# Feed-forward of a two-batch encoder: the last SiLU and product of every first and third chunk are issued behind the next chunk's first copy

## The chip, the cores and the metric

The kernel runs on one core of a Trainium2 chip. The metric is the device time of one execution in microseconds (us). Its engines work side by side, each through its own instructions in a fixed order: TensorE (PE, with its weight loads as PEld), VectorE (DVE), ScalarE (ACT), GpSimd (POOL) and SyncE (SP, which here issues loads).

## The reference, cut to what matters

Two request batches of 512 and 256 tokens (768 rows together, 1024 columns) pass through a trunk of two layers in float32. Each layer is a feed-forward, a token mixer and another feed-forward, so there are four feed-forwards; all share weights between the batches.

```python
def swiglu_ffn(x, w1, w2):                    # w1: 1024 x 5632, w2: 2816 x 1024
    gate, up = jnp.split(x @ w1, 2, axis=-1)
    return (jax.nn.silu(gate) * up) @ w2

for li in range(2):
    x = x + 0.5 * swiglu_ffn(rmsnorm(x, norm_g[li, 0]), ffn_w1[li, 0], ffn_w2[li, 0])
    x = x + mixer(rmsnorm(x, norm_g[li, 1]))  # layer 0: gated recurrence, layer 1: windowed attention
    x = x + 0.5 * swiglu_ffn(rmsnorm(x, norm_g[li, 2]), ffn_w1[li, 1], ffn_w2[li, 1])
```

## The kernel before, in words

Every float32 operand is split into a high part that TensorE takes whole and a low rest, and each product of two operands is three matmuls. The high part of a weight is written by ACT (L203, `CAST w<-wr`), the low part by DVE (L204). Weights are loaded by SP into raw buffers (`wr`); sums of weights are made there too, some by DVE (L217), some by a DMA that adds, issued by POOL (L145, `into`).

The 2816 hidden columns of a feed-forward are 22 chunks of 128. Two are computed plainly (`up_plain`). The rest go through `up_pair`, which computes a chunk's gate and up parts for both halves of the tokens (384 each) with seven products instead of eight, in the order p1, p7, p2, p5, p4, p6, p3. A product is twelve matmuls of 384 columns (L422), summed in one of four PSUM banks a, b, c, d. Behind p1, ACT copies bank a to SBUF (L439), since p2 then goes on summing into the same bank: the first matmul of p2 waits for that copy. Behind p7, ACT copies bank c (L442). At the chunk's end p3 goes to bank d, DVE adds it (L459), ACT takes the SiLU (L460), DVE multiplies (L461), and the result `w` is the chunk's hidden value for the second half of the tokens.

Four chunks make a group. There are five groups in a feed-forward; in group 0 the first two chunks are the plain ones, and two more chunks stand behind the last group. Within a group the chunks go two by two: after each two, `gather` mixes their four values (L351 to L355) and splits the results (L267 on ACT, L268 on DVE). The value `w` of the first chunk of two is read by nothing before that mix, which comes after the second. Behind the four chunks `down_quad` multiplies by the second weights (L486, matmuls of 512 columns, seven products of 18 matmuls), and DVE adds each bank to the residual (L508), which frees the bank.

A recording layer turns this into one order of instructions for each engine. It moves work forward by its own rules; `issue_after(x)` makes what is recorded inside it stand behind `x` on x's engine.

Of the kernel before, what the change touches and what calls it, by code (L numbers as in the profile page):

```python
# [12 lines left out]
AF = mybir.ActivationFunctionType  # L13
# [35 lines left out]
class Trunk:  # L49
    def __init__(self, ctx, tc, consts):  # L50
        self.tc, self.nc = tc, tc.nc
        pool = lambda name, **kw: ctx.enter_context(tc.tile_pool(name=name, bufs=1, **kw))
        self.cp = pool("consts")
        self.xp = pool("xp")
        self.wp = pool("wp")
        self.tp = pool("tp")
        self.sp = pool("stats")
        self.ap = pool("arena")
        self.pp = pool("psum", space=bass.MemoryType.PSUM)
        self.dp = pool("dram", space=bass.MemoryType.DRAM)  # L60
        self.uid = 0
        self.deferred = []
        self.queue, self.loaded, self.staged, self.held = [], [], {}, 0
        self.setup(consts)

# [362 lines left out]
                    skip_group_check=True,  # L428
                )

    def up_pair(self, tag, j):
        nc = self.nc
        key = (tag, j)
        a, b, c, d = (self.ps(H) for _ in range(4))
        v, w, t = (self.tmp(H) for _ in range(3))
        p = lambda name, ps, first, last: self.product(key, name, FACTOR[name], ps, first, last)
        free = lambda *names: [self.done((*key, name)) for name in names]
        p("p1", a, True, False)
        nc.scalar.copy(v, a)  # L439
        free("p1")  # L440
        p("p7", c, True, False)
        nc.scalar.copy(w, c)  # L442
        free("p7")
        p("p2", a, False, True)
        nc.scalar.activation(a, a, AF.Silu)
        free("p2")
        p("p5", d, True, False)
        nc.vector.tensor_sub(w, w, d)
        free("p5")
        p("p4", c, False, True)  # L450
        p("p6", b, True, True)
        nc.vector.tensor_sub(v, v, b)
        nc.vector.tensor_sub(t, c, v)
        nc.vector.tensor_mul(t, t, a)  # L454
        free("p4", "p6")
        yield t
        nc.vector.tensor_sub(w, w, v)
        p("p3", d, False, True)
        nc.vector.tensor_add(v, v, d)  # L459
        self.last_act = nc.scalar.activation(v, v, AF.Silu).ins  # L460
        self.last_dve = nc.vector.tensor_mul(w, v, w).ins  # L461
        free("p3")
        yield w

# [45 lines left out]
    def ffn(self, tag, next_row):  # L510
        for g in range(GROUPS):
            hid = {}

            def put(name, src, kp):
                if name not in hid:
                    hid[name] = self.big([P, 2, 2, H], F32R)
                self.split(src, hid[name][:, kp, 0, :], hid[name][:, kp, 1, :])

            def gather(ts, kp):
                self.mix(ts[0], ts[1], ts[2], ts[3], lambda name, src: put(name, src, kp))  # L520

            if g == 0:
                ts = {}
                for half in range(2):
                    for j in range(PLAIN):
                        t = ts[2 * j + half] = self.up_plain(tag, j, half)
                        name = f"b{j}{half}"
                        if name != "b01":
                            put(name, t, 0)
                gather(ts, 0)  # L530
                self.run_later(len(self.deferred))
            for kp in range(2):
                if g == 0 and kp == 0:
                    continue
                ts = []
                for j in range(2):
                    for half, t in enumerate(self.up_pair(tag, 4 * g + 2 * kp + j)):
                        ts.append(t)
                        name = f"b{j}{half}"
                        if name != "b01":  # L540
                            put(name, t, kp)
                gather(ts, kp)
            self.down_quad(tag, g, hid)
        hids = []
        for j in range(NF - 2, NF):
            hid = self.big([P, 2, T], F32R)
            for half, t in enumerate(self.up_pair(tag, j)):
                self.split(t, *(hid[:, i, half * H : (half + 1) * H] for i in range(2)))
            hids.append(hid)
        if next_row is None:  # L550
            self.load_final()
        banks = {}

        def add(b, k, hid):
            sl = slice(b * P, (b + 1) * P)
            for c in range(2):
                wh, wl = self.take((tag, "last", c))
                if k == 0:
                    banks[(b, c)] = self.ps()
                w = wh[:, k, :], wl[:, k, :]  # L560
                self.mm3(banks[(b, c)], (hid[:, 0, sl], hid[:, 1, sl]), w, k == 0, k == 1)
                if b == NBLK - 1 and k:
                    self.done((tag, "last", c))

        for b in range(NBLK):
            for i, k in (((0, 0), (1, 0), (0, 1)), ((1, 1),))[b] if b < 2 else ((b, 0), (b, 1)):
                add(i, k, hids[k])
            for c in range(2):
                self.add_x(self.x[b][:, c * 512 : (c + 1) * 512], banks[(b, c)], 0.5)
            self.after_block(b, next_row)  # L570
            if b >= 4:
                self.run_later()
# [552 lines left out]
class Unit:  # L1125
# [103 lines left out]
    def finish(self):  # L1229
        lo = self.off + self.b * P  # L1230
        self.k.split(self.po.rearrange("p (c q) -> p c q", c=2), *(t[:, :, lo : lo + P] for t in self.of()))
# [114 lines left out]
```

## Time and profile before

| what | value |
|---|---|
| median of 3 runs | 2763.64 us (2762.39 to 2764.43) |
| the profiled execution | 2764.33 us, its span 2762.5 us |
| granted TensorE clock | 0.999 |
| instructions | 44483 |
| PE busy, PEld busy | 99%, 90% of the span |
| DVE, ACT, POOL busy | 76%, 48%, 11% |

The span is the time from the first to the last instruction of the profile; 1.8 us of the profiled execution lie around it. A matmul's end is modelled, and successive matmuls overlap in the profile, so the row of PE hides short stops; PEld is the row of the weight loads, which run one behind the other where TensorE doesn't wait.

### The profile page before, as it was taken

The numbers are of one execution on the slowest core, as the hardware profiler recorded it, in microseconds if no ns is written. First come the engines' busy times: TensorE is split into PE (matmuls) and PEld (weight loads), VectorE is DVE, ScalarE is ACT, GpSimd is POOL, SyncE is SP. The second block draws the span as 40 slices with busy tenths as digits, with TensorE's granted clock in tenths as the row PEclk, the third lists the DMA queues.
The fourth block names the chain that finished last, engine by engine and source line by source line (L and its number), as shares of the span: only waits on it lengthen the run. The fifth ranks groups of instructions, "written<-read, shape, count | busy, mean of one in ns | idle before, by whom it ended". The sixth has DMA issues, their size and how long they took to land.

```text
span 2762.5 us, 44483 instructions
## 1 busy us (share of the span) xinstructions
PE 2735.5 (99%) x17281; PEld 2481.5 (90%) x17281; DVE 2102.6 (76%) x3662; ACT 1326.6 (48%) x2479; POOL 309.4 (11%) x315
## 2 busy tenths in 40 slices
PE   8999999999999999999999999999999999999998
PEld 8999999888888889999999999999886789999997
DVE  7888788557477568777888878887846768788877
ACT  7444444456466354443446444444546654443444
POOL 1111211000000001121111112111000001221111
PEclk9999999999999999999999999999999999999999
DMA  5544554321110324465444355544512123555443
GB/s 160 135 117 116 138 134 119 118 67 40 55 47 25 122 62 114 112 143 133 118 120 109 83 131 138 133 115 115 146 53 77 47 62 81 134 137 128 120 112 107
DMA packets 330116, 291.63 MB, mean 106 GB/s; under 512 B 11608, under 2 KB 257840, under 8 KB 329904
## 3 DMA queue, kind: packets, MB, share of 16 engines
q1 hardware_dynamic: 294064, 212.43, 25.8%
q0 software_dynamic: 31680, 62.93, 13.4%
q10 hardware_dynamic: 4160, 13.42, 1.4%
q8 instruction: 135, 2.21, 0.3%
q14 instruction: 77, 0.63, 0.1%
HBM read 216.39 MB, written 9.44 MB: 82 GB/s over the span
## 4 chain that ended last, share of the span: by engine, by line
PE 85%; DVE 10%; ACT 3%; issue 2%; DMA 0%; DVEq 0%; ACTq 0%; SPq 0%
PE ps L422 32%; PE ps L486 21%; PE ps L262 9%; PE ps L263 9%; PE ps L264 9%; DVE w L204 2%; DVE big L268 2%; PE ps L682 1%; PE ps L1218 1%; PE ps L1157 1%; PE ps L827 1%; PE ps L1209 1%; ACT w L203 1%; DVE wr L217 1%; PE ps L324 1%
## 5 line engine op out<-in xcount | busy, mean ns | idle before, releaser
L422 PE MATMUL ps<-big,w 128*128 128x384 f32 x6720 | 1174.6, 335 | 3.4 <-ACT tA L439 2.7
L422 PEld LDWEIGHTS ps<-big,w 128*128 128x128 f32 x6720 | 1165.4, 188 | 10.9 <-ACT tA L439 9.1
L203 ACT CAST w<-wr 128x512 fp32r<-128x512 f32 x600 | 415.3, 707 | 699.8 <-DVE wr L217 376.3
L204 DVE TENSOR_TENSOR w<-wr,w 128x512 fp32r<-128x512 f32 (+1 forms) x520 | 452.8, 874 | 180.1 <-ACT w L203 153.9
L486 PE MATMUL ps<-w,big 128*128 128x512 f32 x2520 | 575.9, 389 | 1.2 <-DVE x L508 1.2
L486 PEld LDWEIGHTS ps<-w,big 128*128 128x128 f32 x2520 | 472.4, 188 | 99.6 <-ACT big L267 1.6
L508 DVE SCALAR_TENSOR_TENSOR x<-ps,x 128x512 f32<-128x512 f32 x468 | 303.5, 680 | 10.5 <-PE ps L264 10.0
L145 POOL DMA_DIRECT2D s<-wr x120 | 105.0, 875 | 1667.5 <-DMA wr<-in_ffn_w_dram 784.5
L262 PE MATMUL ps<-w,big 128*128 128x512 f32 x624 | 252.5, 405 | 0.3
L264 PE MATMUL ps<-w,big 128*128 128x512 f32 x624 | 244.6, 392 | 0.9 <-DVE big L331 0.9
L263 PE MATMUL ps<-w,big 128*128 128x512 f32 x624 | 244.4, 392 | 0.0
L262 PE MATMUL ps<-big,w 128*128 128x384 f32 (+2 forms) x640 | 219.2, 344 | 2.1 <-ACT big L267 1.3
L267 ACT CAST big<-tA 128x384 fp32r<-128x384 f32 x296 | 148.0, 513 | 149.3 <-DVE tA L454 69.0
L263 PE MATMUL ps<-big,w 128*128 128x384 f32 (+2 forms) x640 | 216.4, 338 | 0.9 <-DVE big L268 0.6
L264 PE MATMUL ps<-big,w 128*128 128x384 f32 (+2 forms) x640 | 215.6, 337 | 0.0
L268 DVE TENSOR_TENSOR big<-tA,big 128x384 fp32r<-128x384 f32 x296 | 183.0, 629 | 12.7 <-ACT big L267 11.6
L171 DVE TENSOR_TENSOR w<-wr,w 128x1024 fp32r<-128x1024 f32 x92 | 111.8, 1221 | 79.0 <-ACT w L170 73.1
L262 PEld LDWEIGHTS ps<-w,big 128*128 128x128 f32 x624 | 117.2, 188 | 29.3 <-issue 6.0
L170 ACT CAST w<-wr 128x1024 fp32r<-128x1024 f32 x92 | 96.5, 1052 | 97.8 <-PE ps L263 77.8
L204 POOL TENSOR_TENSOR w<-wr,w 128x512 fp32r<-128x512 f32 x80 | 123.3, 1541 | 177.5 <-ACT w L203 156.4
L264 PEld LDWEIGHTS ps<-w,big 128*128 128x128 f32 x624 | 117.1, 188 | 27.6 <-DVE big L331 1.7
L263 PEld LDWEIGHTS ps<-w,big 128*128 128x128 f32 x624 | 117.4, 188 | 21.8 <-issue 0.4
(163 smaller groups left out, 2899.6 us busy)
## 6 DMA issues: line engine op xcount, KB each, us to landing
wr<-in_ffn_w_dram SPq DMA_DIRECT2D x264, 512.0 KB, 3.9
s<-in_ffn_w_dram SPq DMA_DIRECT2D x120, 256.0 KB, 3.3
s<-wr POOLq DMA_DIRECT2D x120, 256.0 KB, 4.5
wr<-wr POOLq DMA_DIRECT2D x80, 256.0 KB, 3.7
wr<-in_hg_w_in_dram SPq DMA_DIRECT2D x40, 512.0 KB, 3.8
wr<-wr POOLq DMA_DIRECT2D x20, 512.0 KB, 4.6
spill<-x ACTq DMA_DIRECT2D x12, 512.0 KB, 2.7
x<-spill ACTq DMA_DIRECT2D x12, 512.0 KB, 3.3
```

The costliest lines, as they stand in the source:

```text
L145: self.nc.gpsimd.dma_start(out, src, accum_op=ALU.add)
L171: self.nc.vector.tensor_sub(lo, raw, hi.bitcast(F32))
L203: nc.scalar.copy(h, src)
L204: low = (eng or nc.vector).tensor_sub(l, src, h.bitcast(F32)).ins
L262: nc.tensor.matmul(out, a[0], b[0], start=first, stop=False)
L263: nc.tensor.matmul(out, a[0], b[1], start=False, stop=False)
L264: nc.tensor.matmul(out, a[1], b[0], start=False, stop=last)
L267: self.nc.scalar.copy(hi, src)
L268: self.nc.vector.tensor_sub(lo, src, hi.bitcast(F32))
L422: self.nc.tensor.matmul(ps, a[x], b[y], start=first and k == 0 and i == 0, stop=k == 3 and i == 2, skip_group_check=True,)
L486: nc.tensor.matmul(ps, a[x], w[y], start=name == chain and kp == 0 and q == 0, stop=kp == 1 and q == 2, skip_group_check=True,)
L508: self.nc.vector.scalar_tensor_tensor(x, ps, c, x, ALU.mult, ALU.add)
```

## The change

`up_pair` gets an argument `hold`, true for the first chunk of each two in a group (the first and third of four; in group 0 the third alone). With it the SiLU and the product (L460, L461 before) are not recorded at the chunk's end but by the next call of `up_pair`, directly behind its first copy, and the SiLU is made to stand behind that copy on ACT. That is 9 chunks in each feed-forward, 36 in the kernel. What is computed stays the same.

```diff
-    def up_pair(self, tag, j):
+    def up_pair(self, tag, j, hold=False):
...
         p("p1", a, True, False)
-        nc.scalar.copy(v, a)
+        turned = nc.scalar.copy(v, a).ins
         free("p1")
+        if self.tail:
+            self.tail(turned)
+        self.tail = None
         p("p7", c, True, False)
...
         p("p3", d, False, True)
         nc.vector.tensor_add(v, v, d)
-        self.last_act = nc.scalar.activation(v, v, AF.Silu).ins
-        self.last_dve = nc.vector.tensor_mul(w, v, w).ins
+
+        def finish(after=None):
+            with self.tc.issue_after(after) if after else nullcontext():
+                self.last_act = nc.scalar.activation(v, v, AF.Silu).ins
+            self.last_dve = nc.vector.tensor_mul(w, v, w).ins
+
+        if hold:
+            self.tail = finish
+        else:
+            finish()
         free("p3")
         yield w
...
-                    for half, t in enumerate(self.up_pair(tag, 4 * g + 2 * kp + j)):
+                    for half, t in enumerate(self.up_pair(tag, 4 * g + 2 * kp + j, j == 0)):
```

On ACT, where the fourth chunk of group 2 begins in the first feed-forward, there stood before (tA are temporaries in SBUF, ps PSUM banks, w and wr split and raw weights, big split operands of the down products):

```order
L203 CAST w_2315<-wr_2262 128x1024
L267 CAST big_1987<-tA_2162 128x384
L460 ACTIVATE tA_2160<-tA_2160 128x384
L439 COPY tA_2299<-ps_2295 128x384
L442 COPY tA_2300<-ps_2297 128x384
L203 CAST w_2345<-wr_2264 128x1024
L445 ACTIVATE ps_2295<-ps_2295 128x384
```

The same place now, where the new lines shift line numbers (L440 is the copy L439 of before, L467 the SiLU, L446 the second copy, L268 and L204 the casts L267 and L203):

```order
L204 CAST w_2313<-wr_2262 128x1024
L268 CAST big_1987<-tA_2162 128x384
L440 COPY tA_2297<-ps_2293 128x384
L467 ACTIVATE tA_2160<-tA_2160 128x384
L446 COPY tA_2298<-ps_2295 128x384
L204 CAST w_2345<-wr_2264 128x1024
L449 ACTIVATE ps_2293<-ps_2293 128x384
```

The SiLU and the copy have changed places, and nothing else. On ACT, where the second chunk of the same group begins, there stood before (`s` is the buffer in which a DMA adds two weights):

```order
L267 CAST big_1987<-tA_1879 128x384
L460 ACTIVATE tA_1877<-tA_1877 128x384
L439 COPY tA_2013<-ps_2009 128x384
L203 CAST w_2029<-s_278_1866 128x512
L442 COPY tA_2014<-ps_2011 128x384
```

and now:

```order
L268 CAST big_1987<-tA_1879 128x384
L440 COPY tA_2011<-ps_2007 128x384
L204 CAST w_2027<-s_278_1866 128x512
L467 ACTIVATE tA_1877<-tA_1877 128x384
L446 COPY tA_2012<-ps_2009 128x384
```

Here the SiLU has moved past the copy and past one cast of a weight. DVE at this second place had before:

```order
L268 TENSOR_TENSOR big_1987<-tA_1879,big_1987 128x384
L461 TENSOR_TENSOR tA_1878<-tA_1877,tA_1878 128x384
L204 TENSOR_TENSOR w_2029<-s_278_1866,w_2029 128x512
L204 TENSOR_TENSOR w_2045<-wr_1862,w_2045 128x512
L448 TENSOR_TENSOR tA_2014<-tA_2014,ps_2012 128x384
```

and has now:

```order
L269 TENSOR_TENSOR big_1987<-tA_1879,big_1987 128x384
L205 TENSOR_TENSOR w_2027<-s_278_1866,w_2027 128x512
L468 TENSOR_TENSOR tA_1878<-tA_1877,tA_1878 128x384
L205 TENSOR_TENSOR w_2045<-wr_1862,w_2045 128x512
L452 TENSOR_TENSOR tA_2012<-tA_2012,ps_2010 128x384
```

The product has moved behind one subtraction of a weight. That is so at 19 of the 36 places; at the other 17 DVE's order is unchanged. The orders of PE, POOL and SP are the same in both kernels.

More of the change, by code (lines that the diff above doesn't have):

```diff
@@ L438, in up_pair @@
         p("p1", a, True, False)
-        nc.scalar.copy(v, a)
+        turned = nc.scalar.copy(v, a).ins
         free("p1")
+        if self.tail:
+            self.tail(turned)
+        self.tail = None
         p("p7", c, True, False)
```

## The prediction

> **What bounds the kernel now.** I read the page first, then who waited for whom, then three places by time. In the page's rows of engines and of costly groups (count, then busy us, mean ns, idle us and what ended it) TensorE is the bound:
>
> ```profile
> span 2762.5 us, 44483 instructions
> PE 2735.5 (99%) x17281; PEld 2481.5 (90%) x17281; DVE 2102.6 (76%) x3662; ACT 1326.6 (48%) x2479; POOL 309.4 (11%) x315
> L422 PE MATMUL ps<-big,w 128*128 128x384 f32 x6720 | 1174.6, 335 | 3.4 <-ACT tA L439 2.7
> L422 PEld LDWEIGHTS ps<-big,w 128*128 128x128 f32 x6720 | 1165.4, 188 | 10.9 <-ACT tA L439 9.1
> ```
>
> So a gain must come from stops of PE, and the change touches one kind of stop only: p2's first matmul waiting for the copy L439. The waits of PE and of its weight loads give its size (us in total, times, longest), and the one other wait that matters below:
>
> ```profile
> PE ps L422 <- ACT tA L439: 2.7, 11, 0.4
> PEld ps L422 <- ACT tA L439: 9.1, 19, 0.8
> PE ps L486 <- DVE x L508: 1.2, 1, 1.2
> ```
>
> **What a stop costs.** Here is the start of the fourth chunk of group 2, first feed-forward (start, duration, idle time before it and who ended that):
>
> ```profile
> 247.20 0.52 ACT L267 CAST big<-tA 128x384 fp32r<-128x384 f32 x1 [0.46 <-DVE tA L454]
> 247.74 0.55 DVE L459 TENSOR_TENSOR tA<-tA,ps 128x384 f32<-128x384 f32 x1
> ...
> 248.32 0.53 ACT L460 ACTIVATE tA<-tA 128x384 f32<-128x384 f32 x1 [0.61 <-DVE tA L459]
> ...
> 248.75 0.46 ACT L439 COPY tA<-ps 128x384 f32<-128x384 f32 x1
> 249.21 0.48 ACT L442 COPY tA<-ps 128x384 f32<-128x384 f32 x1
> 249.27 10.38 PEld L422 LDWEIGHTS ps<-big,w 128*128 128x128 f32 x60 [0.47 <-ACT tA L439]
> 249.27 10.69 PE L422 MATMUL ps<-big,w 128*128 128x384 f32 x60 [0.15 <-ACT tA L439]
> 249.59 1.06 ACT L203 CAST w<-wr 128x1024 fp32r<-128x1024 f32 x1
> 249.81 0.55 DVE L461 TENSOR_TENSOR tA<-tA,tA 128x384 f32<-128x384 f32 x1
> 250.85 0.88 POOL L145 DMA_DIRECT2D wr<-wr  x1 [10.89 <-ACT w L203]
> ```
>
> ACT is done with L267 at 247.72, then stands idle 0.61 us because the SiLU is next and DVE's L459 ends only at 248.29. The copy's bank was ready long before (p7's twelve matmuls, 2.1 us, lie between p1 and the p2 that is due at 248.96 by the next lines, so p1 ended near 246.9); it starts behind the SiLU and ends at 249.21; p2 starts 0.06 later. The pace of matmuls is (10.38 - 0.19) / 59 = 0.173 us, while one lasts 0.335 in the profile, so the last matmul before the stop began at 249.27 - 0.15 - 0.335 = 248.79, the next was due at 248.96, and the stop costs 0.31 us: PE's idle time plus 0.16, or the load's idle time minus 0.16. Over all stops that is 9.1 - 19 x 0.16 = 6.1 us. PE's own row counts only the 11 longer ones, 2.7 + 11 x 0.16 = 4.5, which leaves about 0.2 for each of the eight short ones; the sum of 6.1 is consistent and I take it.
>
> The Trainium skill bears on this choice of row: "Perfetto Trace Analysis", section "Identifying the Most-Contended Engine", says that the busy share of matmuls is a poor measure because they are pipelined, and that the busy share of weight loads should be used. Taken literally the gain would be all 9.1 us. The trace agrees with half of it: the matmul row does understate (0.15 for 0.31), but the load row overstates by as much (0.47).
>
> **The change, part by part.** *The copy goes ahead of the SiLU.* It can start when ACT ends L267, at 247.72, and ends 0.46 later at 248.18. PE's p2 is due at 248.96, so 0.78 us are to spare and the stop goes. I take the 19 stops of the row to have this cause, since all wait for the same line. Price: -6.1 us, and its bounds are 4.5 (the eleven that PE's row counts) and 9.1 (all idle time of the loads).
>
> *The SiLU goes behind the copy.* In this place it needs L459, which ends at 248.29, after the copy. So it starts at 248.32 as before, ends at 248.85, and L442, whose product p7 now ends unstopped (its copy can start about 249.14), doesn't wait for it. L461 on DVE stood behind a longer subtraction anyway. Price 0.
>
> *Where the second chunk follows the first* there is no stop today:
>
> ```profile
> 218.15 0.55 DVE L459 TENSOR_TENSOR tA<-tA,ps 128x384 f32<-128x384 f32 x1
> 218.27 0.51 ACT L267 CAST big<-tA 128x384 fp32r<-128x384 f32 x1 [1.63 <-DVE tA L454]
> ...
> 218.73 0.53 ACT L460 ACTIVATE tA<-tA 128x384 f32<-128x384 f32 x1
> 219.16 0.46 ACT L439 COPY tA<-ps 128x384 f32<-128x384 f32 x1
> 219.22 0.55 DVE L268 TENSOR_TENSOR big<-tA,big 128x384 fp32r<-128x384 f32 x1
> 219.52 0.62 ACT L203 CAST w<-s 128x512 fp32r<-128x512 f32 x1
> 219.69 0.55 DVE L461 TENSOR_TENSOR tA<-tA,tA 128x384 f32<-128x384 f32 x1
> ...
> 220.17 0.69 DVE L204 TENSOR_TENSOR w<-s,w 128x512 fp32r<-128x512 f32 x1
> ```
>
> The copy moves to 218.78, the cast to about 219.2, the SiLU to 219.8 with its end at 220.3. DVE does the subtraction (220.17) 0.4 us earlier and the product (219.69) 0.6 us later; the two add up to the same busy time. The DMAs of SP and POOL that reuse `s` wait for that subtraction, so they come earlier if anything. Nothing reads the product before the mix, a whole chunk later. Price 0; its bounds are 0 and the 0.6 us that the third rival takes.
>
> *What is late next.* With PE 0.31 us earlier from p2 on, the down stage begins earlier, but the chain that feeds it does not:
>
> ```profile
> 253.76 0.55 DVE L448 TENSOR_TENSOR tA<-tA,ps 128x384 f32<-128x384 f32 x1 [0.80 <-PE ps L422]
> 255.57 1.05 ACT L203 CAST w<-wr 128x1024 fp32r<-128x1024 f32 x1 [3.42 <-DMA wr<-wr]
> 256.66 1.23 DVE L204 TENSOR_TENSOR w<-wr,w 128x1024 fp32r<-128x1024 f32 x1 [2.35 <-ACT w L203]
> 257.92 0.55 DVE L452 TENSOR_TENSOR tA<-tA,ps 128x384 f32<-128x384 f32 x1
> 259.80 4.51 PE L486 MATMUL ps<-w,big 128*128 128x512 f32 x19
> 262.55 0.68 DVE L508 SCALAR_TENSOR_TENSOR x<-ps,x 128x512 f32<-128x512 f32 x1
> ```
>
> L203 waits here for a DMA that POOL issued at 250.85, behind the cast of 249.59, behind L442. That cast moves only from 249.59 to about 249.52, so DVE's L452 moves 0.07 where PE moves 0.31, and the first L508 comes 2.75 + 0.24 = 2.99 us after the down stage's start instead of 2.75. How late may it come? One group shows the limit, and the last group of the kernel is near it:
>
> ```profile
> 1247.88 2.00 ACT L203 CAST w<-wr 128x1024 fp32r<-128x1024 f32 x2 [5.56 <-DMA wr<-wr]
> 1249.97 4.28 PE L486 MATMUL ps<-w,big 128*128 128x512 f32 x18
> 1254.63 0.68 DVE L508 SCALAR_TENSOR_TENSOR x<-ps,x 128x512 f32<-128x512 f32 x1
> 1255.46 6.86 PE L486 MATMUL ps<-w,big 128*128 128x512 f32 x29 [1.20 <-DVE x L508]
> ```
>
> ```profile
> 2680.21 16.00 PE L486 MATMUL ps<-w,big 128*128 128x512 f32 x69
> 2683.38 0.68 DVE L508 SCALAR_TENSOR_TENSOR x<-ps,x 128x512 f32<-128x512 f32 x1
> ```
>
> In the late group ACT waited for the DMA 2.1 us longer (5.56 against 3.42), L508 came 4.66 us after the start, and PE, due again at 1249.97 + 18 x 0.229 = 1254.09, went on at 1255.46: a stop of 1.37. So up to 4.66 - 1.37 = 3.29 us are free. 2.99 stays below that. In the late group the stop grows by 0.2, and the last group (3.17 now, 3.5 then) gets one of 0.2 to 0.3. I charge 0.5 for both.
>
> **The sum.** -6.1 + 0.5 = -5.6 us: from the profiled execution's 2764.33 to 2758.7. The median shown is 0.7 us below that execution, so 2763.64 - 5.6 = 2758.0, which is 0.20% and stands exactly at the 0.2% that a measurement of this kernel can just tell from no change.
>
> **The rivals.** *The down stage gives it back.* If L508 had no reserve, each of the 19 stops would keep only what the cast of L203 gains: 0.07 us above, more where a longer stop held L442 too. At 0.1 each that is 1.9: 2761.7. For it speaks how often ACT waits for such a landing:
>
> ```profile
> ACT w L203 <- DMA wr<-wr: 124.0, 33, 5.6
> ```
>
> Against: the 0.54 us between 2.75 and 3.29. It decides where L508 comes later than 3.29, or if landings are some 0.3 us later than here.
>
> *It doesn't do what it says:* PE's wait would be for another event that ends with the copy, such as p2's weights or the bank. Then 2763.6. Against: p2 starts 0.06 us behind the copy's end, and no row shows PE waiting for a weight in L422.
>
> *Slower: DVE held up by the late product.* At the 19 places where DVE's order changes, the product stands at DVE's head until the SiLU ends, 0.6 us later than now. If each reached PE, 19 x 0.6 = 11.4 less 5.6 gives 2769.4. It decides from the point where L448 ends after p3 is due: L448 ends at 254.31, and p3 starts at 249.27 + 48 x 0.173 = 257.6, so over 3 us are to spare. Nothing in the profile speaks for it.
>
> *All idle time of the loads is time:* 9.1 - 0.5 = 8.6 us, 2755.0. This is the skill's rule above; the pace of 0.173 speaks against it.
>
> **Chances.** Forecast 0.72, of which 0.43 lie beyond 0.2% and 0.29 within, since its sum is known to some 0.8 us (landings of DMAs vary, and the 0.5 may be 0 or 1.5). Given back 0.13, no effect 0.06, slower 0.04, the larger gain 0.05. So faster by over 0.2%: 0.43 + 0.05 = 0.48; within: 0.29 + 0.13 + 0.06 = 0.48; slower 0.04. The range goes from 2756.2 (6.1 us kept whole, and 1.4 less in a late group) to 2761.8 (given back, 2761.7), and leaves out 0.15.
>
> **What would show it.** In the profile after, PE's and PEld's waits for the first copy of a chunk should be gone from L422, and ACT's row order be copy, SiLU, second copy with the copy ending near 0.8 us ahead of p2. The first residual add of a down stage should come about 3.0 us after its start, and the wait of L486 for it show two or three times with some 2 us in all. The prediction is wrong if that wait grows to many places, if DVE's L448 begins to come late, or if p2 still starts late with the copy done.

## The result and the profile after

The changed kernel takes 2759.77 us (median of 22 runs, 2758.11 to 2761.64) against 2764.49 us for the kernel before (22 runs, 2762.39 to 2767.02). The ratio is 0.9981 with a 95% interval of 0.9975 to 0.9986: 4.7 us, or 0.19%, faster. The forecast was 5.6 us less. The time fell inside the range, but the two terms behind the 5.6 were both wrong in size, in opposite directions.

The profiled execution after took 2760.57 us. These are its rows on the page (span, engines) and in the view of groups of instructions; in a group's row, after the count, stand busy us, mean ns and idle us, the same as in the rows shown of before. L423 is the up products' line now, L498 the down products', L520 the residual add (L422, L486 and L508 before).

```profile
span 2758.8 us, 44483 instructions
PE 2733.7 (99%) x17281; PEld 2481.9 (90%) x17281; DVE 2100.5 (76%) x3662; ACT 1327.5 (48%) x2479; POOL 309.2 (11%) x315
...
L423 PE MATMUL ps<-big,w 128*128 128x384 f32 x6720 | 1169.2, 334 | 0.0
L423 PEld LDWEIGHTS ps<-big,w 128*128 128x128 f32 x6720 | 1165.9, 188 | 1.6
L498 PE MATMUL ps<-w,big 128*128 128x512 f32 x2520 | 579.0, 390 | 2.0 <-DVE x L520 1.9
L498 PEld LDWEIGHTS ps<-w,big 128*128 128x128 f32 x2520 | 471.0, 188 | 104.8 <-ACT big L268 4.5 <-DVE x L520 3.4
```

Busy and idle time of a group together are the time that TensorE spends in that stage. The up products took 1174.6 + 3.4 = 1178.0 us before (rows in the prediction) and take 1169.2 now: 8.8 less. No wait for the copy is left. For the down products the rows of before, not shown yet, are

```profile
L486 PE MATMUL ps<-w,big 128*128 128x512 f32 x2520 | 575.9, 389 | 1.2 <-DVE x L508 1.2
L486 PEld LDWEIGHTS ps<-w,big 128*128 128x128 f32 x2520 | 472.4, 188 | 99.6 <-ACT big L267 1.6 <-DVE x L508 0.5
```

so by PE's row they took 577.1 and take 581.0: 3.9 more. Counted from the start of one matmul to the start of the next, the two differences are the same (8.8 less, 3.9 more). Together they make -4.9, and the spans differ by 3.7. The remaining 1.2 lies in the stages that the change doesn't touch; two traces of the kernel before differ there by as much. Here is the place of the prediction's third block of lines, the start of the fourth chunk of group 2, by time:

```profile
246.35 0.51 ACT L268 CAST big<-tA 128x384 fp32r<-128x384 f32 x1 [0.47 <-DVE tA L458]
246.77 0.47 ACT L440 COPY tA<-ps 128x384 f32<-128x384 f32 x1
246.89 0.55 DVE L463 TENSOR_TENSOR tA<-tA,ps 128x384 f32<-128x384 f32 x1
247.36 0.55 DVE L269 TENSOR_TENSOR big<-tA,big 128x384 fp32r<-128x384 f32 x1
247.48 0.53 ACT L467 ACTIVATE tA<-tA 128x384 f32<-128x384 f32 x1 [0.24 <-DVE tA L463]
...
248.31 0.48 ACT L446 COPY tA<-ps 128x384 f32<-128x384 f32 x1 [0.31 <-PE ps L423]
248.69 1.06 ACT L204 CAST w<-wr 128x1024 fp32r<-128x1024 f32 x1
```

The copy L440 follows the cast at once, the SiLU L467 starts where L463 lets it, as before, and the second copy now waits for PE. The first copy ends at 247.24, 0.8 us ahead of p2's first matmul (248.06 in the trace). Each of these was forecast.

### The profile page after: what moved, and what is told of

Same layout as the page of the kernel before. It is cut to its first block, busy times and chain, and to the rows that moved or that the text cites. A ratio compares the mean times of both kernels' runs of the same rounds, so it can differ in the third digit from the quotient of the medians.

```text
span 2758.8 us, 44483 instructions
## 1 busy us (share of the span) xinstructions
PE 2733.7 (99%) x17281; PEld 2481.9 (90%) x17281; DVE 2100.5 (76%) x3662; ACT 1327.5 (48%) x2479; POOL 309.2 (11%) x315
## 4 chain that ended last, share of the span: by engine, by line
PE 95%; DVE 2%; ACT 2%; DMA 1%; issue 0%; DVEq 0%; SPq 0%; ACTq 0%
PE ps L423 41%; PE ps L498 20%; PE ps L263 9%; PE ps L265 9%; PE ps L264 9%; PE ps L694 1%; PE ps L1230 1%; PE ps L1169 1%; PE ps L839 1%; PE ps L1221 1%; PE ps L325 1%; DMA wr<-wr 1%; PE ps L815 0%; DVE x L520 0%; ACT big L328 0%
## 5 line engine op out<-in xcount | busy, mean ns | idle before, releaser
L423 PE MATMUL ps<-big,w 128*128 128x384 f32 x6720 | 1169.2, 334 | 0.0
L423 PEld LDWEIGHTS ps<-big,w 128*128 128x128 f32 x6720 | 1165.9, 188 | 1.6
L204 ACT CAST w<-wr 128x512 fp32r<-128x512 f32 x600 | 415.1, 706 | 707.4 <-DVE wr L218 371.6
L498 PE MATMUL ps<-w,big 128*128 128x512 f32 x2520 | 579.0, 390 | 2.0 <-DVE x L520 1.9
L498 PEld LDWEIGHTS ps<-w,big 128*128 128x128 f32 x2520 | 471.0, 188 | 104.8 <-ACT big L268 4.5
L520 DVE SCALAR_TENSOR_TENSOR x<-ps,x 128x512 f32<-128x512 f32 x468 | 303.6, 683 | 10.2 <-PE ps L265 10.0
L268 ACT CAST big<-tA 128x384 fp32r<-128x384 f32 x296 | 148.1, 513 | 162.2 <-DVE tA L458 76.8
```

What stands on the lines that cost most here:

```text
L204: nc.scalar.copy(h, src)
L268: self.nc.scalar.copy(hi, src)
L423: self.nc.tensor.matmul(ps, a[x], b[y], start=first and k == 0 and i == 0, stop=k == 3 and i == 2, skip_group_check=True,)
L498: nc.tensor.matmul(ps, a[x], w[y], start=name == chain and kp == 0 and q == 0, stop=kp == 1 and q == 2, skip_group_check=True,)
L520: self.nc.vector.scalar_tensor_tensor(x, ps, c, x, ALU.mult, ALU.add)
```

## The experiments

All were run on the chip, each beside runs of the kernel before. The trace was read the same way each time: PE's time in the two groups of rows above, busy plus idle.

**Which chunks bring it.** The last line of the diff is the only edit in each of these two.

```diff
-                    for half, t in enumerate(self.up_pair(tag, 4 * g + 2 * kp + j, j == 0)):
+                    for half, t in enumerate(self.up_pair(tag, 4 * g + 2 * kp + j, j == 0 and kp == 1)):   # e1_third
+                    for half, t in enumerate(self.up_pair(tag, 4 * g + 2 * kp + j, j == 0 and kp == 0)):   # e2_first
```

> Only the third chunks of the groups hand their SiLU and product on (20 places); the first chunks finish as before. Theory: the gain comes from these places alone, so the time is that of the changed kernel, 4.5 to 5 us below before (some 2759.8), and the two traces agree in the down stages. Rival, that moving the product at the first chunks has a price or a gain of its own: more than 1 us away from the changed kernel.

> Only the first chunks of groups 1 to 4 hand on (16 places), where TensorE had no stop. Theory: the time is that of before within 0.5 us, and the weight loads' wait for the copy stays near 9 us. Rival, that DVE held up by the later product costs PE time: slower than before by 1 us or more (0.6 us at up to 16 places).

The third chunks alone gave 2759.67 us (11 runs) beside 2765.15 for before, ratio 0.9980 (0.9971 to 0.9989). The first chunks alone gave 2764.25 us (11 runs), ratio 0.9997 (0.9988 to 1.0006), no difference. In the groups' rows, e1_third first, then e2_first:

```profile
L423 PE MATMUL ps<-big,w 128*128 128x384 f32 x6720 | 1169.6, 334 | 0.0
L423 PEld LDWEIGHTS ps<-big,w 128*128 128x128 f32 x6720 | 1165.8, 188 | 2.1 <-ACT tA L440 0.3
...
L498 PE MATMUL ps<-w,big 128*128 128x512 f32 x2520 | 579.0, 390 | 2.2 <-DVE x L520 2.1
```

```profile
L423 PE MATMUL ps<-big,w 128*128 128x384 f32 x6720 | 1174.2, 334 | 3.5 <-ACT tA L440 3.0
L423 PEld LDWEIGHTS ps<-big,w 128*128 128x128 f32 x6720 | 1165.4, 188 | 10.6 <-ACT tA L440 9.1
L498 PE MATMUL ps<-w,big 128*128 128x512 f32 x2520 | 576.0, 389 | 1.1 <-DVE x L520 1.1
```

e1_third reads like the changed kernel (1169.6 and 581.2), e2_first like the one before (1177.7 and 577.1, and the loads still wait 9.1 us for the copy). So all but some 0.4 us of the effect sits where the fourth chunk follows the third. The 0.4 us (1169.6 for 1169.2) are a few short waits for the copy in second chunks, 0.3 us in the loads' row of e1_third. Moving the product at the first chunks shows no cost: the rival of a DVE held up by it falls.

**Whether the sum of two down weights gives the gain back.** The down stage needs a21 + a22, two quarters of the second weights. It is added by a DMA that POOL issues in the chunk before the down stage. Here DVE adds it instead, in an otherwise idle moment of that chunk, once in the changed kernel and once in the one before.

```diff
-        self.into(a21, a22)
+        if up:
+            self.into(a21, a22)
...
         sums = {"p6": (a11, a21), "p3": (a12, a11)}
+        if not up:
+            sums["p5"] = (a21, a22)
```

> The changed kernel, with the sum of two down weights (a21 += a22, 20 times) made by DVE where the chunk before the down stage has idle DVE time, and no longer by a DMA that POOL issues. Theory, that the landing of this DMA is what gives part of the gain back: all 20 down stages take 28.4 us, PE's waits for L508's line vanish, and the time is 1.5 to 4 us below the changed kernel, some 2756 to 2758. Rival, that the residual adds come late because DVE has too much to do: 20 x 1.2 us more on DVE make it as slow as the changed kernel or slower.

> The kernel before, with the same sum on DVE. Theory: it had little to lose there (1.9 us over all down stages in the profile shown), so 0.5 to 2 us below before, about 2763, and the distance to the same edit on the changed kernel is the whole of the stops, 6.1 us. Rival, that the stops at the copy were only partly lost time: a distance of 4.7 us, as between the two kernels without this edit.

With it the changed kernel takes 2754.91 us (5 runs, 2753.41 to 2755.57), ratio to before 0.9962 (0.9949 to 0.9974). The kernel before takes 2763.97 us (11 runs), ratio 0.9995 (0.9986 to 1.0004), not told apart from no change. The groups of e3_after_dve, then of e4_before_dve:

```profile
L426 PE MATMUL ps<-big,w 128*128 128x384 f32 x6720 | 1169.2, 334 | 0.0
...
L501 PE MATMUL ps<-w,big 128*128 128x512 f32 x2520 | 575.3, 389 | 0.0
```

```profile
L425 PE MATMUL ps<-big,w 128*128 128x384 f32 x6720 | 1174.6, 335 | 3.8 <-ACT tA L442 3.3
L425 PEld LDWEIGHTS ps<-big,w 128*128 128x128 f32 x6720 | 1165.2, 188 | 11.4 <-ACT tA L442 9.7
L489 PE MATMUL ps<-w,big 128*128 128x512 f32 x2520 | 575.3, 389 | 0.0
```

The first is below the 2756 to 2758 expected. The down products take 575.3 us in both, with no stop, and each of the 20 down stages takes 28.60 us (28.4 was expected), although DVE got 20 more instructions of 1.22 us. So it was the landing of this DMA, and not a busy DVE, that took 581.0 - 575.3 = 5.7 us in the changed kernel and 1.8 before. Of the two stages only the up products still differ: 1178.4 - 1169.2 = 9.2 us in the rows. The medians differ by 9.06. Neither theory had that: I had written 6.1, and the rival 4.7. The stops had cost half as much again as I had charged.

**Whether only the moment of that sum counts.** POOL adds it with an instruction of its own, and DVE's order stays that of the changed kernel.

```diff
-        self.into(a21, a22)
+        if up:
+            self.into(a21, a22)
+        else:
+            nc.gpsimd.tensor_add(a21, a21, a22)
```

> The changed kernel, with the sum of two down weights (a21 += a22, 20 times) made by POOL itself, and no longer by a DMA that POOL issues; DVE's order stays that of the changed kernel. Theory, that only the moment counts at which this sum is there: by the 1.5 us that POOL takes for half the size it is there some 2 us earlier than the DMA's, so the down stages all take 28.4 us and the time is that of the kernel with the sum on DVE, within 1 us of 2755. Rival, that it was DVE's changed order that helped there: the time stays near the changed kernel's 2759.8.

It takes 2754.6 us (5 runs, 2753.47 to 2755.15), ratio 0.9961 (0.9947 to 0.9975), the same as with DVE. Its groups, and POOL's additions in the view by line:

```profile
L426 PE MATMUL ps<-big,w 128*128 128x384 f32 x6720 | 1169.2, 334 | 0.0
L501 PE MATMUL ps<-w,big 128*128 128x512 f32 x2520 | 575.3, 389 | 0.0
```

```profile
L196 POOL TENSOR_TENSOR wr<-wr,wr 128x1024 f32<-128x1024 f32 x20 | 48.3, 2413 | 201.0 <-DVE tA L471 73.3 <-DMA wr<-in_ffn_w_dram 69.9 <-ACT w L207 50.0
```

For comparison, DVE's addition in e3_after_dve by time, and the DMA in the changed kernel by the page's list of DMA issues (number, size, median us from issue to landing):

```profile
250.70 1.22 DVE L221 TENSOR_TENSOR wr<-wr,wr 128x1024 f32<-128x1024 f32 x1
```

```profile
wr<-wr POOLq DMA_DIRECT2D x20, 512.0 KB, 4.6
```

An addition of 2.4 us by POOL or of 1.22 us by DVE does, where the DMA needed 4.6. Both versions of the changed kernel are about 10 us faster than the kernel before, and about 5 faster than the changed one (2759.77, and 2760.56 in one run beside the second version). So it was not DVE's changed order that helped. Both versions also take a transfer of 512 KB out of each of the 20 groups; no run separates this from the earlier sum.

**Both kernels once more.** A second trace of each, unchanged.

> The changed kernel once more, for a second trace. Theory: no stop at any first copy; the first residual add of a down stage comes some 0.45 us later than before in nearly all groups (median near 3.2 us), and each down stage is longer by what that goes beyond 3.0 us, 2 to 6 us over all 20, other groups being hit than in the first trace. Rival, that something fixed in the program makes some groups late: the same groups with the same times.

> The kernel before once more, for a second trace. Theory: the stops at the copy make the fourth chunks of groups longer by some 8.8 us over all, of which the idle time of the matmul row plus one overlap counts only 6.1, and the down stages lose 0.2 to 2 us. Rival, that the 8.8 us are particular to one trace: nearer to 6.

The changed kernel took 2760.56 us, its groups 1169.2 and 579.5 + 1.9 = 581.4. The one before took 2765.14 us, its groups 1174.4 + 3.3 = 1177.7 and 575.9 + 1.1 = 577.0. So 8.5 us at the stops and 4.4 given back are those of a second pair of traces, and the rival of a figure nearer to 6 falls. In the changed kernel's second trace the median group has its first residual add 3.17 us after its start, and each down stage is longer by what that goes beyond 3.0 us, as expected. On which groups are late the expectation was half wrong. The third group of the second feed-forward is late in every trace with the DMA. PE there, by time, in the changed kernel's first and second trace:

```profile
1247.64 4.28 PE L498 MATMUL ps<-w,big 128*128 128x512 f32 x18
1253.09 24.94 PE L498 MATMUL ps<-w,big 128*128 128x512 f32 x108 [1.17 <-DVE x L520]
```

```profile
1248.56 4.28 PE L498 MATMUL ps<-w,big 128*128 128x512 f32 x18
1254.51 1.85 PE L498 MATMUL ps<-w,big 128*128 128x512 f32 x7 [1.67 <-DVE x L520]
```

So that landing is some 2 us late at the same place of the program each time; what delays it stays open. The last group of the kernel is late in every one of these traces too, by less (28.77 us and 28.78 before, 29.17 and 29.08 after, for 28.60). The first groups of the second, third and fourth feed-forward never are: they had no stop at the copy before. Which of the others are late differs from trace to trace.

## Why the prediction was right, point by point

*The bound and the cause* were right: PE's stops at p2's first matmul came from the copy queued behind a SiLU, and they are gone. e1_third and e2_first put nearly all of them where the prediction had them. Of the 19 waits of the row, 17 stood at the start of a fourth chunk; three chunks had none there. The matmuls also show three short stops of 0.1 us each in second chunks, where the prediction saw none.

*What a stop costs* was mis-sized, 6.1 us charged and 8.8 measured. The failing step is "the load's idle time minus 0.16". The prediction's own rows held the rest: p2 started at 249.27 and the down stage at 259.80, which is 10.53 us for 60 matmuls. In the trace after, with no stop, the last 30 matmuls ahead of the down stage (at 258.46) take 5.20 us, so 60 take 10.40:

```profile
253.26 5.36 PE L423 MATMUL ps<-big,w 128*128 128x384 f32 x30
```

Some 0.13 us more were lost behind the restart. By the starts of single matmuls in the trace before, the step was 0.49 us at the stop, 0.28 at the next matmul, 0.17 to 0.19 at the six behind it, and then 0.173 again. In running order the load starts ahead of its matmul (259.63 and 259.80 at the start of the down stage); behind the wait the first load and the first matmul begin together (249.27 both). That the lost lead causes the slow restart is a reading, which no run tests. So this stop cost about 0.31 + 0.13 = 0.44, close to the 0.47 us of idle time in the row of the loads, and the chunk became 0.45 shorter (15.01 us before, 14.56 after). The bound of 9.1 us, which I had kept as the upper end and as a rival with a chance of 0.05, was close to the size of the term. The Trainium skill ("Perfetto Trace Analysis", section "Identifying the Most-Contended Engine") advises to judge TensorE's headroom by its weight loads and not by its matmul row. For the up products this fits: the loads' row had 9.1, PE's row 2.7, and the stage became 8.8 shorter. For the down products it doesn't, as shown below.

*What is late next* was the right mechanism (the down stage starts earlier than its feed) and mis-sized too, 0.5 us charged and 3.9 measured. Two steps failed. The first was that the DMA would be issued 0.07 us earlier, since its row named the cast before it as what ended the wait. In the changed kernel that cast ends at 248.69 + 1.06 = 249.75, and POOL issues only at 250.40; before, the cast ended at 250.65 and POOL issued at 250.85. POOL first waits for ACT and for a load; these semaphore waits stand in the trace, but not in the views shown. That wait is over at 250.20 before, while the cast is still running, and at 249.75 now, 0.65 ahead of the issue both times. An SP wait for the same load is over at the same times (250.19 and 249.74). So what ends POOL's wait is the landing of the other raw weight, whose load SP issues some 4 us ahead. In the rows of SP and POOL by time, before and then after:

```profile
246.73 0.37 SPq L155 DMA_DIRECT2D wr<-in_ffn_w_dram  x1
```

```profile
245.88 0.37 SPq L156 DMA_DIRECT2D wr<-in_ffn_w_dram  x1
...
250.40 0.88 POOL L146 DMA_DIRECT2D wr<-wr  x1 [11.29 <-ACT w L204]
```

From SP's issue to POOL's it is 4.12 us before and 4.52 after; before, the cast can have no part in it. SP issues that load 0.03 us after DVE ends a subtraction early in the chunk (246.70 before, 245.85 after). So the chain follows the chunk's start, and not p2, while the down stage begins a whole 0.45 earlier. In this group the load also took 0.40 longer than before; over the 20 groups POOL issues at a median of 6.17 us after the chunk's start before and 6.25 after.

The second failing step was the reserve, "up to 3.29 us are free". It counts the late group's stop up to 1255.46 and nothing behind it; but the 108 matmuls from there to 1280.24 took 24.78 us, where at 28.60 / 126 each they take 24.51. Group 2 of the changed kernel shows what such a reading misses: PE's row has no stop in the stage, and the loads' row has two (PE and DVE, then PEld by time):

```profile
258.46 29.17 PE L498 MATMUL ps<-w,big 128*128 128x512 f32 x126
...
261.87 0.68 DVE L520 SCALAR_TENSOR_TENSOR x<-ps,x 128x512 f32<-128x512 f32 x1
...
287.47 1.75 PE L423 MATMUL ps<-big,w 128*128 128x384 f32 x9
```

```profile
262.67 9.84 PEld L498 LDWEIGHTS ps<-w,big 128*128 128x128 f32 x44 [0.35 <-ACT big L268]
272.83 14.38 PEld L498 LDWEIGHTS ps<-w,big 128*128 128x128 f32 x64 [0.32 <-DVE x L520]
```

Before, by the time of PE's rows there, the stage ran from 259.80 to the next chunk's start:

```profile
288.40 1.92 PE L422 MATMUL ps<-big,w 128*128 128x384 f32 x10
```

and in the late group of the prediction it ended at

```profile
1280.24 1.92 PE L422 MATMUL ps<-big,w 128*128 128x384 f32 x10
```

In group 2 that is 28.60 us with the first residual add 2.75 after its start, and now 29.01 with the add 3.41 after it. The stage is 0.41 longer and the add 0.41 beyond 3.0. In the late group the add came 4.66 after the start at 1249.97 and the stage took 30.27: 1.67 longer, 1.66 beyond 3.0. So 3.0 us were free, not 3.29; all 40 down stages of the changed kernel's two traces follow this within 0.06 us. The residual add is a mark here and not the only cause: the first of the two waits is for the cast L268, which is late with it. With 0.45 on top of 2.75, and landings that vary, 13 of the 20 groups go beyond 3.0 in the first trace and 12 in the second, 2 before. PE's idle row doesn't show it: L498 has 2.0 us of idle time for 3.9 us lost. The loads' row shows where they are, as waits for L520 and for the cast L268, but it overstates: these rise from 0.5 and 1.6 to 3.4 and 4.5, 5.8 us together. In this stage the loads don't run one behind the other: they stand idle 99.6 us even before, nearly all of it while PE runs on, so their idle time is no price there.

*The signs* show the same trap. PE's waits for the residual add came three times with 1.9 us, about as forecast, while the loads had 12 such waits where 2 stood before. That was the sign of being wrong, and only the loads' row gave it:

```profile
PE ps L498 <- DVE x L520: 1.9, 3, 1.2
PEld ps L498 <- DVE x L520: 3.4, 12, 0.3
```

*The rivals.* The one with the down stage giving the gain back took place in good part: 3.9 of 8.8 us. The one without effect fell with the trace after, the slower one with e2_first, in which the product is later and neither stage moves. The one by the loads' row was nearly right on its term; its time was not reached since the give-back was larger too.

*The sum.* -8.8 + 3.9 = -4.9 where -6.1 + 0.5 = -5.6 stood. Two errors of 2.7 and 3.4 us nearly cancelled, so the forecast was close by luck in its sizes, though its mechanism held. The experiments with the sum on DVE take them apart: without the give-back the change is worth 9.1 us.

## What to carry to other kernels

Size a short stop of TensorE from the length of its stage with it and without it. Here the matmul row hid more than half of the loss; the idle time of the weight loads was close in the up products, where loads else run without a gap, and too high in the down products, where they don't. When an edit takes a stop away, look for the chain that does not move with the engine that now runs ahead: here a transfer tied to a buffer released earlier took back 3.9 of 8.8 us, and replacing it with an addition of 1.22 or 2.4 us on an engine with idle time brought about as much again as the edit. On the kernel before, the same replacement brought nothing that could be told from no change. Where a transfer waits for several events, compare its issue with each of them in two traces before trusting the one that the row names.

## What the runs showed of the hardware that was not expected

The wait for one copy cost about 0.45 us where the matmul row shows 0.15 idle: behind the wait the first weight load and the first matmul begin together (249.27 both), and the matmuls that follow lose another 0.13 us before they are back at their pace. And one of the 20 landings of the accumulating DMA was some 2 us late in every trace that had it, at the same place in the program; no run tells why.
